# A conditioning vector loaded as eight packed columns and spread over the partitions by TensorE, with nine warming products instead of fourteen

## The chip, the cores and the metric

The kernel runs on one core of a Trainium2 chip. The metric is the device time of one execution in microseconds (us). The time before is 2213.28 us, the median of three runs that lie between 2211.96 and 2214.94 us.

## What is computed

The kernel is a trunk of two residual layers over one sequence of 1024 tokens with 1024 channels: layer 0 mixes tokens by multi-head latent attention, layer 1 by an mLSTM matrix memory, and each is followed by a gated MLP with a causal width-3 convolution. Every sub-layer normalises its input and shifts, scales and gates it by numbers that depend on a conditioning vector `c` of 1024 elements. What matters here is the head of it:

```
c_act = jax.nn.silu(c)
for i in range(DEPTH):
    mod = c_act @ mod_w[i] + mod_b[i]
    sh_a, sc_a, g_a, sh_f, sc_f, g_f = split(mod, 6)
    h = rms_norm(x) * (1 + sc_a) + sh_a
    ...  # attention or mLSTM, starting with h @ w_in
```

So no product of the first projection `h @ w_in` can be formed before the scale `sc_a` of its channels is known, and that needs `silu(c)` and the rows of `mod_w` for those channels.

## The kernel before

Activations lie with channels on the 128 partitions (P) and tokens along the free dimension, so that 1024 channels are eight tiles, counted by `k`. Products are made in three terms from a rounded high part and a rest: a helper (`mm3`, lines 171 to 182) issues high times high (L175), rest of the moving operand times high (L176) and high times rest of the weight (L177).

The first projection is made k by k, while its operands arrive. `load_k(k)` (L330 to L336) issues three DMAs on SyncE's queue: `sraw`, the 128 x 1024 block of `mod_w` that gives the scale of the channels of tile k; `wraw`, the 128 x 896 weights; and `x`, the first 512 tokens of tile k. `prepare(k)` (L338 to L345) then does, for one k:

- on VectorE (DVE) `mod_dot` (L198), which multiplies `sraw` by `crow` and sums along the row, and `mod_bias` (L203), which adds the bias column from `cols`: together they give the scale of the channels;
- on ScalarE (ACT) the rounded weights `winh` (L343), on DVE the rest `winl` (L345);
- in `scaled` on ACT the rounded scaled input (the first of the two tiles named `h`, L351), on DVE its rest (the second `h`, L352).

`in_k` (L354 to L359) issues 21 products for one k, seven output tiles `ia` times three terms. ACT also squares `x` for the normalisation (`ssq`, `sq`, L240 and L243), DVE adds the squares up (L245). The factor from the normalisation is applied only when the finished projection is read out of PSUM.

`crow` is `silu(c)` repeated on all 128 partitions, since `mod_dot` needs it along the free dimension on each. Before, a broadcast DMA (L134) writes c 128 times, 512 KB in all, as the first transfer of the program, and ACT applies the Silu in place (L135). `cols` holds small per-channel vectors (biases, gains, and so on) packed as columns; `load_cols(0, ...)` loads the first part of it (L156), from within `load_k(0)`.

Two more pieces lie in the same stretch. Fourteen products of the identity with itself (`warm`, L409) keep TensorE busy from the program's start, with no use for their result. `rope_tables` (L365 to L389) loads the positions by four small DMAs behind `load_k(1)` and works out angles with six ACT instructions (L372 to L377), DVE instructions (L378 to L382) and three sines; its result is needed only after the projection.

The order on each engine is set by a scheduler of the language's tile layer, not by hand: it may place an instruction ahead of one that is written earlier. In the trace of before each engine runs its own list from top to bottom, and an instruction that waits holds up all that stand behind it on that engine.

Of the kernel before, what the change touches and what calls it, by code (L numbers as in the profile page):

```python
# [11 lines left out]
F32 = mybir.dt.float32  # L12
F32R = mybir.dt.float32r
I32 = mybir.dt.int32
AF = mybir.ActivationFunctionType
# [3 lines left out]
P = 128  # L19
D = 1024  # L20
S = 1024
KT = D // P
HS = 512
# [16 lines left out]

STEPS = "nspppnspppoooonmooso", "nnsposppooponpmspoopo"
XW = (4, 2)
WARM = 14
W0, W0_RSTD, WF, WF_RSTD = (6, 10), (4, 3), (4, 5), (4, 4)
SHARE = 7
GATES = (2, 16, 20, 24)
# [14 lines left out]

_W = [("mb0", 48), ("mb1", 48), ("qn", 4), ("kvn", 2), ("hn", 8), ("fn", 8), ("invf", 1), ("mg", 3), ("gb", 2),
      ("cw0", 66), ("cb0", 22), ("cw1", 66), ("cb1", 22)]
COL = {}
_o = 0
# [30 lines left out]
def trunk_kernel(ctx: ExitStack, tc: tile.TileContext, xT, pos, c_d, cols_d, mod_w, win, winT, w0, w1, wf, wd, out):  # L98
    nc = tc.nc
# [3 lines left out]
    def nm(s):  # L103
        n_names[0] += 1
        return f"{s}_{n_names[0]}"

    act, dve, pool, pe = nc.scalar, nc.vector, nc.gpsimd, nc.tensor

    cst = ctx.enter_context(tc.tile_pool(name="cst", bufs=1))
# [19 lines left out]
    def block(i, shape, dt, name):  # L129
        return blk.tile(shape, dt, tag=f"b{i}", name=nm(name))  # L130


    crow = cst.tile([P, D], F32, name="crow")
    nc.sync.dma_start(crow, c_d.broadcast_to([P, D]))  # L134
    act.activation(crow, crow, AF.Silu)  # L135
    cols = [cst.tile([P, COLS[0][1]], F32, name="cols"), None, None]
    ident = cst.tile([P, P], F32, name="ident")
    make_identity(nc, ident)
# [13 lines left out]
    def load_cols(i, p):  # L152
        a, b = COLS[i]
        if i > 0:
            cols[i] = p.tile([P, b - a], F32, name=f"cols{i}")
        nc.sync.dma_start(cols[i], cols_d[:, a:b])  # L156

    def mm_tile(name):
        return psA.tile([P, HS], F32, tag="mm", name=nm(name))
# [164 lines left out]
    def load_x(hf, k):  # L324
        nc.sync.dma_start(xs[hf][:, k, :], xT[k, :, hf * HS:(hf + 1) * HS])

    def small(name):
        return psS.tile([P, HS], F32, tag="sm", bufs=1, name=nm(name))

    def load_k(k):  # L330

        nc.sync.dma_start(sraw[:, k % 4, :], mod_w[0, 8 + k])
        if k == 0:
            load_cols(0, cst)
        nc.sync.dma_start(wraw[:, k % 4, :], win[k])
        load_x(0, k)  # L336

# [27 lines left out]
    def rope_tables(scr):  # L365

        Q = S // 4
        ang, n, n1, n2, t, pi = [scr[:, i * Q:(i + 1) * Q] for i in range(6)]
        pi = pi.bitcast(I32)
        for i in range(4):  # L370
            nc.sync.dma_start(pi[32 * i:32 * i + 32, :], pos[:, i * Q:(i + 1) * Q].broadcast_to([32, Q]))
        act.activation(ang, pi, AF.Copy, scale=col("invf"))  # L372
        act.activation(n, ang, AF.Identity, scale=1.0 / TWO_PI, bias=col("mg"))
        act.activation(n, n, AF.Identity, bias=col("mg", 1))
        act.activation(n1, n, AF.Identity, scale=1.0 / 2048.0, bias=col("mg"))
        act.activation(n1, n1, AF.Identity, bias=col("mg", 1))
        act.activation(n1, n1, AF.Copy, scale=2048.0)  # L377
        dve.tensor_tensor(n2, n, n1, ALU.subtract)  # L378

        for v, part in ((n1, PI1), (n2, PI1), (n1, PI2), (n2, PI2), (n, PI3)):  # L380
            dve.scalar_tensor_tensor(ang, v, -part, ang, ALU.mult, ALU.add)
        dve.tensor_scalar(ang, ang, -PI_IN, PI_IN, ALU.max, ALU.min)  # L382
        act.activation(t, ang, AF.Abs)
        act.activation(n, t, AF.Sin, scale=-1.0, bias=col("mg", 2))
        act.activation(n1, ang, AF.Sin)
        act.activation(n2, ang, AF.Sin, scale=-1.0)
        cs_d = dram.tile([3, 4, 32, Q], F32, name="csd")
        act.dma_start(cs_d.rearrange("i q f t -> (q f) i t"), scr[:, Q:4 * Q].rearrange("p (i t) -> p i t", i=3))
        return cs_d  # L389
# [14 lines left out]
        rstd_later(ssq[hf], D, ssq[hf], keep_rb, XW[hf], small)  # L404


    ps = small("warm")
    for _ in range(WARM):
        pe.matmul(ps[:, 0:P], ident, ident, start=True, stop=True)  # L409


    load_k(0)
    load_k(1)
    cs_d = rope_tables(block(1, [P, 6 * 256], F32, "rt"))
    load_k(2)
    load_k(3)
    prepare(0)
# [405 lines left out]
    for n in range(2 * NH):  # L823
        q, kk, qr, kvu, i, hf, head = args.pop(0)
# [694 lines left out]
    for t in range(8):  # L1519
        ps = mm_tile("vp")  # L1520
# [7 lines left out]
    gi, gf, gb, gc = [g1[:, i * P:(i + 1) * P] for i in range(4)]  # L1528
# [156 lines left out]
def _units(w):  # L1685

    k, m = w.shape
    return w.reshape(k // P, P, m // P, P).transpose(2, 1, 0, 3).reshape(m // P, P, k)


def _cols(v):
    return v.reshape(-1, P).T


def arrange(inputs):
    a = {k: np.asarray(v) for k, v in inputs.items()}
    f = np.float32
    xT = np.ascontiguousarray(a["x"][0].T).reshape(KT, P, S)
    pos = np.ascontiguousarray(a["positions"][0].reshape(1, S))

    cols = np.zeros((P, NCOL), f)

    def put(name, v):
        cols[:v.shape[0], COL[name]:COL[name] + v.shape[1]] = v

    for l in range(2):
        put(f"mb{l}", _cols(a["mod_b"][l]))
        cw = a["ffn_conv_w"][l]
        put(f"cw{l}", cw.reshape(3, FT, P).transpose(2, 1, 0).reshape(P, FT * 3))
        put(f"cb{l}", _cols(a["ffn_conv_b"][l]))  # L1710
    put("qn", _cols(a["mla_q_norm"][0]))
    put("kvn", _cols(a["mla_kv_norm"][0]))
    put("hn", _cols(a["ml_head_norm"][0]))
    put("fn", _cols(a["final_norm"]))
    invf = np.array(INVF, f)
    put("invf", np.tile(invf, 4)[:, None])
    put("mg", np.tile(np.array([[MAGIC, -MAGIC, math.pi / 2]], f), (P, 1)))
    put("gb", np.repeat(a["ml_b_gates"][0].reshape(2, MH).T, NC, axis=0))

    wi = a["mla_w_in"][0]  # L1720
    win = np.concatenate([wi, wi[:, 768:]], axis=1).reshape(KT, P, 896)
    winT = np.ascontiguousarray(win.reshape(D, 896).T).reshape(7, P, D)

    mod_w = np.ascontiguousarray(a["mod_w"].transpose(0, 2, 1)).reshape(2, 48, P, D)
    wq = a["mla_w_q_up"][0].reshape(512, NH, 192)
    wkv = a["mla_w_kv_up"][0].reshape(256, NH, 256)
    w0 = np.empty((18, P, 1024), f)
    for g in range(4):
        for i in range(2):
            w0[U_QN + g, :, i * 512:(i + 1) * 512] = _units(np.ascontiguousarray(wq[:, 2 * g + i, :128]))[0]  # L1730
            w0[U_KV + g, :, i * 256:(i + 1) * 256] = _units(np.ascontiguousarray(wkv[:, 2 * g + i, :128]))[0]
        w0[U_QR + g // 2, :, (g % 2) * 512:(g % 2 + 1) * 512] = _units(
            np.concatenate([wq[:, 2 * g, 128:], wq[:, 2 * g + 1, 128:]], axis=1))[0]
        wv = np.concatenate([wkv[:, 2 * g, 128:], wkv[:, 2 * g + 1, 128:]], axis=1)
        w0[U_KV + g, :, 512:] = wv.reshape(2, P, 256).transpose(1, 0, 2).reshape(P, 512)
    w0[U_OUT0:U_OUT0 + 8] = _units(a["mla_w_out"][0])

    wm = a["ml_w_in"][0]
    w1 = np.empty((33, P, 1024), f)
    w1[U_MQ:U_MQ + 8] = _units(wm[:, 0:1024])  # L1740

    wg = np.concatenate([wm[:, 1024:1280], wm[:, 3072:]], axis=1).reshape(KT, P, 264).transpose(1, 0, 2)
    for i, u in enumerate(U_MV0):
        part = wg[:, 3 * i:3 * i + 3].reshape(P, -1)
        w1[u, :, :part.shape[1]] = part
        w1[u, :, part.shape[1]:] = 0
    for i in range(1, MH):
        wv = wm[:, 1024 + i * 256:1024 + (i + 1) * 256].reshape(2, 4, P, 256)
        w1[U_MV + 2 * i:U_MV + 2 * i + 2] = wv.transpose(0, 2, 1, 3).reshape(2, P, 1024)
    w1[U_MO:U_MO + 8] = _units(wm[:, 2048:3072])  # L1750
    w1[U_OUT1:U_OUT1 + 8] = _units(a["ml_w_out"][0])

    wf = np.empty((2, FT, 2, P, 1024), f)
    wd = np.empty((2, KT, P, FT * P), f)
    for l in range(2):
        up = _units(a["ffn_w_up"][l])
        wf[l, :, 0] = up[:FT]
        wf[l, :, 1] = up[FT:]
        wd[l] = _units(a["ffn_w_down"][l])
    return [("xT", xT), ("pos", pos), ("c", a["c"]), ("cols", cols), ("mod_w", mod_w), ("win", win),  # L1760
            ("winT", winT), ("w0", w0), ("w1", w1),
            ("wf", wf), ("wd", wd)]
# [16 lines left out]
```

## Time and profile before

| what | value |
|---|---|
| median of three runs | 2213.28 us |
| the profiled execution's own time | 2209.6 us |
| its span, first to last instruction | 2207.8 us |
| TensorE (PE) busy | 2165.6 us, 98% of the span |
| VectorE (DVE) busy | 1697.9 us, 77% |
| ScalarE (ACT) busy | 1045.3 us, 47% |
| mean granted TensorE clock | 0.996 |
| PE's share of the chain that ended last | 85% |

PE is TensorE, PEld its weight loads, SPq the queue on which SyncE issues DMAs. A line such as L198 is a line of the kernel. In a timeline the first number is the start in us from the start of the span, the second how long the row took; in brackets stands the idle time ahead of it and what ended it. The rows of a DMA issue show the issue alone; the time to landing is a view of its own. The profiled execution's time lies 1.8 us above its span and 3.7 us below the median of the three runs.

### The profile page before, as it was taken

The page shows a single profiled execution, that of the slowest core. Times are in us where ns is not written, and L with a number is a line of the kernel's source. Part 1 is how long each engine was busy: PE and PEld are TensorE (multiplying, and loading weights), DVE is VectorE, ACT ScalarE, POOL GpSimd, SP SyncE. Part 2 cuts the span into 40 slices and gives each one's busy share as a digit, 9 for nine tenths or more (in the row PEclk, how much of TensorE's full clock was granted, in tenths as well). Part 3 has the DMA queues.
Part 4 walks back from the last instruction along what each step waited for, and adds up shares of the span by engine and source line. Part 5 has one row for each costly group of instructions (what it writes and reads, how often), then busy time and mean ns, then how long its engine had stood idle before and what let it go on. Part 6 is the DMA issues. An engine that isn't in the chain of part 4 may idle for free.

```text
span 2207.8 us, 28744 instructions
## 1 busy us (share of the span) xinstructions
PE 2165.6 (98%) x10557; PEld 1817.1 (82%) x10557; DVE 1697.9 (77%) x2753; ACT 1045.3 (47%) x1812; POOL 200.5 (9%) x232
## 2 busy tenths in 40 slices
PE   9999999999999999999999999999999999999998
PEld 7878888787888888778888888988788888877887
DVE  8877788669878776999974754566887777779987
ACT  6456566456444444443353434354554444453335
POOL 0000000000000000242210111010000000022232
PEclk9999999999999999999999999999999999999999
DMA  8512334832444432543133332354233332245122
GB/s 316 156 47 67 94 102 156 278 115 74 151 143 138 134 130 80 191 150 95 51 115 105 102 124 77 114 172 158 68 134 100 110 116 95 78 155 208 45 79 77
DMA packets 105085, 270.50 MB, mean 123 GB/s; under 512 B 12336, under 2 KB 15984, under 8 KB 104944
## 3 DMA queue, kind: packets, MB, share of 16 engines
q1 hardware_dynamic: 104544, 268.28, 36.8%
q8 instruction: 83, 1.36, 0.2%
q14 instruction: 58, 0.48, 0.1%
q10 hardware_dynamic: 400, 0.39, 0.1%
HBM read 221.53 MB, written 44.47 MB: 120 GB/s over the span
## 4 chain that ended last, share of the span: by engine, by line
PE 85%; DVE 8%; DMA 2%; ACT 2%; issue 1%; POOL 0%; SPq 0%; DVEq 0%; POOLq 0%; ACTq 0%
PE pa L177 7%; PE pa L175 7%; PE pa L176 7%; PE pd L175 4%; PE pd L176 4%; PE pd L177 4%; PE sc L677 3%; PE da L175 3%; PE da L177 3%; PE da L176 3%; PE op L175 3%; PE op L177 2%; PE op L176 2%; PE inp L177 2%; PE inp L175 2%; PE db L177 2%
## 5 line engine op out<-in xcount | busy, mean ns | idle before, releaser
L992 ACT ACTIVATE whi<-raw 128x512 fp32r<-128x512 f32 (+1 forms) x252 | 147.5, 607 | 262.3 <-PE pb L176 61.0
L992 ACT ACTIVATE whi<-wsum 128x512 fp32r<-128x512 f32 (+1 forms) x224 | 133.9, 617 | 184.5 <-PE pa L176 61.5
L175 PE MATMUL pa<-T,whi 128*128 128x512 f32 x528 | 206.3, 391 | 5.0 <-DVE g L1080 5.0
L177 PE MATMUL pa<-T,wlo 128*128 128x512 f32 x528 | 206.1, 390 | 3.1 <-DVE wlo L993 3.1
L176 PE MATMUL pa<-T,whi 128*128 128x512 f32 x528 | 205.7, 390 | 0.0
L993 DVE TENSOR_TENSOR wlo<-wsum,whi 128x512 fp32r<-128x512 f32 (+1 forms) x224 | 150.6, 685 | 33.7 <-ACT whi L992 32.2
L993 POOL TENSOR_TENSOR wlo<-raw,whi 128x512 fp32r<-128x512 f32 (+1 forms) x96 | 140.8, 1480 | 382.5 <-ACT whi L992 341.8
L175 PE MATMUL da<-U,whi 128*128 128x512 f32 (+1 forms) x364 | 139.8, 384 | 2.2 <-ACT whi L992 2.2
L176 PE MATMUL da<-U,whi 128*128 128x512 f32 (+1 forms) x364 | 139.2, 382 | 0.0
L177 PE MATMUL da<-U,wlo 128*128 128x512 f32 (+1 forms) x364 | 138.5, 382 | 0.0
L167 ACT ACTIVATE whi<-wraw 128x1024 fp32r<-128x1024 f32 x67 | 70.7, 1058 | 112.7 <-PE op L176 60.2
L993 DVE TENSOR_TENSOR wlo<-raw,whi 128x512 fp32r<-128x512 f32 (+1 forms) x156 | 104.7, 678 | 24.4 <-ACT whi L992 24.4
L175 PEld LDWEIGHTS pa<-T,whi 128*128 128x128 f32 x528 | 99.3, 188 | 28.0 <-DVE g L1080 4.1
L177 PEld LDWEIGHTS pa<-T,wlo 128*128 128x128 f32 x528 | 99.3, 188 | 24.5 <-DVE wlo L993 4.0
L176 PEld LDWEIGHTS pa<-T,whi 128*128 128x128 f32 x528 | 99.3, 188 | 20.4
L1143 DVE TENSOR_TENSOR U<-q,U 128x1024 fp32r<-128x1024 f32 x84 | 108.2, 1306 | 6.0 <-ACT U L1142 5.5
L1032 ACT ACTIVATE ct<-a,cols 128x512 f32<-128x512 f32 x88 | 71.0, 808 | 87.5 <-DVE a L1054 47.8
L168 DVE TENSOR_TENSOR wlo<-wraw,whi 128x1024 fp32r<-128x1024 f32 x67 | 82.4, 1233 | 37.0 <-ACT whi L167 34.9
L177 PE MATMUL db<-U,wlo 128*128 128x512 f32 x264 | 102.7, 390 | 1.7 <-DVE wlo L993 1.7
L175 PE MATMUL db<-U,whi 128*128 128x512 f32 x264 | 103.7, 393 | 0.0
L176 PE MATMUL db<-U,whi 128*128 128x512 f32 x264 | 102.8, 390 | 0.0
L175 PE MATMUL op<-oh,whi 128*128 128x512 f32 x256 | 100.1, 391 | 1.0 <-ACT oh L731 1.0
(378 smaller groups left out, 6078.5 us busy)
## 6 DMA issues: line engine op xcount, KB each, us to landing
raw<-in_wf SPq DMA_DIRECT2D x96, 512.0 KB, 4.1
wraw<-in_w SPq DMA_DIRECT2D x67, 512.0 KB, 3.6
mraw<-in_mod_w SPq DMA_DIRECT2D x56, 512.0 KB, 3.6
ud<-ct SPq DMA_DIRECT2D x88, 256.0 KB, 2.3
q<-ud SPq DMA_DIRECT2D x88, 256.0 KB, 4.1
raw<-in_wd SPq DMA_DIRECT2D x32, 512.0 KB, 5.7
pa<-in_mod_w SPq DMA_DIRECT2D x24, 512.0 KB, 3.6
x<-xd SPq DMA_DIRECT2D x48, 256.0 KB, 4.4
```

Of the source, the lines that this page charges most:

```text
L167: act.activation(hi, raw, AF.Copy)
L168: dve.tensor_tensor(lo, raw, hi.bitcast(F32), ALU.subtract)
L175: pe.matmul(ps, lh, rh, start=first, stop=False, skip_group_check=more)
L176: pe.matmul(ps[:, 0:rl.shape[-1]], lh, rl, start=False, stop=False, skip_group_check=more)
L177: pe.matmul(ps, ll, rh, start=False, stop=last, skip_group_check=more)
L677: pe.matmul(ps[:, cs], a[:, qs if n < 3 else qrs_], b[:, cs], start=n == 0, stop=n == 4)
L992: act.activation(hi, src, AF.Copy)
L993: eng.tensor_tensor(lo, src, hi.bitcast(F32), ALU.subtract)
L1032: act.activation(t, a[:, 2:], AF.Identity, bias=col(f"cb{l}", m), scale=cw(m, 2))
L1143: dve.tensor_tensor(lo, w, hi.bitcast(F32), ALU.subtract)
```

## The change

`c` is put into the host-side array `cols` as eight columns of 128 (the table `_W` and one `put`), so that it arrives with `cols`. That load is issued first, and the broadcast of 512 KB at the program's start goes away. ACT applies the Silu to the 128 x 8 block (`ccol`). TensorE then makes `crow` in eight transposes: each takes one column, repeated along the free dimension, as a 128 x 128 operand, and writes its 128 elements as a row on all partitions of PSUM (`cr`, two tiles of four transposes). ACT copies the first half to `crow`, DVE the second. The fourteen warming products become four ahead of the transposes and five behind them, and the two `load_k` calls move ahead of them in the text. Two later broadcasts of c (L1513 and L1655) stay.

```
-WARM = 14
+WARM, WARM2 = 4, 5
...
-_W = [..., ("mg", 3), ("gb", 2),
+_W = [..., ("mg", 3), ("gb", 2), ("c", 8),
...
     crow = cst.tile([P, D], F32, name="crow")
-    nc.sync.dma_start(crow, c_d.broadcast_to([P, D]))
-    act.activation(crow, crow, AF.Silu)
...
     def load_k(k):
         nc.sync.dma_start(sraw[:, k % 4, :], mod_w[0, 8 + k])
-        if k == 0:
-            load_cols(0, cst)
         nc.sync.dma_start(wraw[:, k % 4, :], win[k])
         load_x(0, k)
...
+    load_cols(0, cst)
+    load_k(0)
+    load_k(1)
     ps = small("warm")
     for _ in range(WARM):
         pe.matmul(ps[:, 0:P], ident, ident, start=True, stop=True)
-    load_k(0)
-    load_k(1)
+    ccol = cst.tile([P, KT], F32, name="ccol")
+    act.activation(ccol, cols_at(COL["c"], KT), AF.Silu)
+    for i in range(2):
+        cr = mm_tile("cr")
+        for t in range(4):
+            pe.transpose(cr[:, t * P:(t + 1) * P], ccol[:, i * 4 + t:i * 4 + t + 1].to_broadcast([P, P]), ident)
+        if i:
+            dve.tensor_copy(crow[:, HS:], cr)
+        else:
+            act.activation(crow[:, 0:HS], cr, AF.Copy)
+    for _ in range(WARM2):
+        pe.matmul(ps[:, 0:P], ident, ident, start=True, stop=True)
     cs_d = rope_tables(block(1, [P, 6 * 256], F32, "rt"))
...
+    put("c", _cols(a["c"][0]))
```

The scheduler lays out the first stretch anew. ACT's list before, at the very start of the program (the first `winh`, `h`, `ssq` belong to tile k = 0, the second `winh` and `h` and the `sq` to k = 1, `rt` to the rope tables):

```order
L135 ACTIVATE crow<-crow 128x1024
L343 ACTIVATE winh_98<-wraw_97 128x896
L351 ACTIVATE h_94<-x_93,modc_79 128x512
L240 ACTIVATE ssq_114<-x_93 128x512
L343 ACTIVATE winh_100<-wraw_97 128x896
L351 ACTIVATE h_94<-x_93,modc_79 128x512
L243 ACTIVATE sq_195<-x_93 128x512
L372 ACTIVATE rt_138<-rt_138,cols 128x256
```

ACT's list in the changed kernel, from its first `winh`, which follows the Silu of `ccol` (line numbers stand two to four lower than before, here L339 for L343, L347 for L351, L368 to L373 for L372 to L377):

```order
L339 ACTIVATE winh_96<-wraw_95 128x896
L238 ACTIVATE ssq_112<-x_91 128x512
L339 ACTIVATE winh_98<-wraw_95 128x896
L241 ACTIVATE sq_202<-x_91 128x512
L419 ACTIVATE crow<-cr_128 128x512
L368 ACTIVATE rt_145<-rt_145,cols 128x256
L369 ACTIVATE rt_145<-rt_145,cols 128x256
L370 ACTIVATE rt_145<-rt_145,cols 128x256
L371 ACTIVATE rt_145<-rt_145,cols 128x256
L372 ACTIVATE rt_145<-rt_145,cols 128x256
L373 ACTIVATE rt_145<-rt_145 128x256
L347 ACTIVATE h_92<-x_91,modc_77 128x512
```

The copy into `crow` stands behind the weights and the squares of both k = 0 and k = 1, and the first `h` has moved from third place to behind the six rope instructions.

DVE's list before, at the same place (`modc` is the column of scales, the `h` written here is the rest of the scaled input):

```order
L198 SCALAR_TENSOR_TENSOR sraw_96,modc_79<-sraw_96,crow 128x1024
L203 SCALAR_TENSOR_TENSOR modc_79<-modc_79,cols 128x1
L345 TENSOR_TENSOR winl_99<-wraw_97,winh_98 128x896
L352 SCALAR_TENSOR_TENSOR h_95<-x_93,modc_79,h_94 128x512
L198 SCALAR_TENSOR_TENSOR sraw_96,modc_79<-sraw_96,crow 128x1024
```

DVE's list in the changed kernel, from its first instruction:

```order
L341 TENSOR_TENSOR winl_97<-wraw_95,winh_96 128x896
L341 TENSOR_TENSOR winl_99<-wraw_95,winh_98 128x896
L417 COPY crow<-cr_134 128x512
L243 TENSOR_TENSOR ssq_112<-ssq_112,sq_202 128x512
L196 SCALAR_TENSOR_TENSOR sraw_94,modc_77<-sraw_94,crow 128x1024 x2
L201 SCALAR_TENSOR_TENSOR modc_77<-modc_77,cols 128x1
L196 SCALAR_TENSOR_TENSOR sraw_94,modc_77<-sraw_94,crow 128x1024
L374 TENSOR_TENSOR rt_145<-rt_145 128x256
L377 SCALAR_TENSOR_TENSOR rt_145<-rt_145 128x256
L348 SCALAR_TENSOR_TENSOR h_93<-x_91,modc_77,h_92 128x512
```

The first scale (L201) now stands behind two weight rests, a copy, an addition of squares and two dots, where it stood behind one dot.

PE's list in the changed kernel, from its first instruction; before, fourteen `warm` were followed at once by L175, L176, L177 for each `ia` in turn:

```order
L408 MATMUL warm_121<-ident 128x128 x4
L415 MATMUL cr_128<-ident,ccol 128x128 x4
L415 MATMUL cr_134<-ident,ccol 128x128 x4
L421 MATMUL warm_121<-ident 128x128 x5
L173 MATMUL ia_181<-h_92,winh_96 128x512
L173 MATMUL ia_182<-h_92,winh_96 128x512
L173 MATMUL ia_183<-h_92,winh_96 128x512
L173 MATMUL ia_184<-h_92,winh_96 128x512
```

All seven products that need only the high part of the first `h` have moved ahead of those that need its rest. Beyond this the lists of ACT, DVE, PE and SyncE differ in some places up to the first scores of the attention, where the second half of the projection is normalised, and agree after that.

More of the change, by code (lines that the diff above doesn't have):

```diff
@@ L60 @@
 HB = ((4, 3), (1, 5))
-_W = [("mb0", 48), ("mb1", 48), ("qn", 4), ("kvn", 2), ("hn", 8), ("fn", 8), ("invf", 1), ("mg", 3), ("gb", 2),
+_W = [("mb0", 48), ("mb1", 48), ("qn", 4), ("kvn", 2), ("hn", 8), ("fn", 8), ("invf", 1), ("mg", 3), ("gb", 2), ("c", 8),
       ("cw0", 66), ("cb0", 22), ("cw1", 66), ("cb1", 22)]
```

## The prediction

> **What bounds the kernel now.** I read the page first, then the timeline of the first 20 us, then stretches of the span with their granted clock, then PE's waits. The page:
>
> ```profile
> span 2207.8 us, 28744 instructions
> PE 2165.6 (98%) x10557; PEld 1817.1 (82%) x10557; DVE 1697.9 (77%) x2753; ACT 1045.3 (47%) x1812; POOL 200.5 (9%) x232
> ```
>
> TensorE (PE) stands still for 42 us in all, so a change in the head acts only through when PE's useful work begins. The timeline shows that start (first number: start, second: length):
>
> ```profile
> 1.45 6.22 PE L409 MATMUL warm<-ident 128*128 128x128 f32 x28 [1.45 <-POOL ident masks.py:199]
> 3.91 0.44 SPq L335 DMA_DIRECT2D wraw<-in_win  x1
> 4.39 0.47 SPq L325 DMA_DIRECT2D x<-in_xT  x1
> 5.12 1.06 ACT L135 ACTIVATE crow<-crow 128x1024 f32<-128x1024 f32 x1 [3.04 <-DMA crow<-in_c]
> 6.70 1.23 DVE L198 SCALAR_TENSOR_TENSOR sraw<-sraw,crow 128x1024 f32<-128x1024 f32 x1 [6.70 <-DMA sraw<-in_mod_w]
> 7.90 0.95 ACT L343 ACTIVATE winh<-wraw 128x896 fp32r<-128x896 f32 x1 [1.73 <-DMA wraw<-in_win]
> 7.96 0.16 DVE L203 SCALAR_TENSOR_TENSOR modc<-modc,cols 128x1 f32<-128x1 f32 x1
> 8.76 0.71 ACT L351 ACTIVATE h<-x,modc 128x512 fp32r<-128x512 f32 x1
> 8.88 1.09 DVE L345 TENSOR_TENSOR winl<-wraw,winh 128x896 fp32r<-128x896 f32 x1 [0.76 <-ACT winh L343]
> 9.51 0.50 PE L175 MATMUL ia<-h,winh 128*128 128x512 f32 x1 [1.84 <-ACT h L351]
> 9.89 0.75 DVE L352 SCALAR_TENSOR_TENSOR h<-x,modc,h 128x512 fp32r<-128x512 f32 x1
> 12.46 0.63 PE L177 MATMUL ia<-h,winl 128*128 128x512 f32 x1
> 12.89 0.63 PE L175 MATMUL ia<-h,winh 128*128 128x512 f32 x1
> 16.71 0.39 PE L177 MATMUL ia<-h,winl 128*128 128x512 f32 x1
> 16.94 0.39 PE L175 MATMUL ia<-h,winh 128*128 128x512 f32 x1
> ```
>
> The Silu of c ends at 6.2 us, before the first dot starts: that dot waits for its own weights, not for c. The first product starts at 9.51, the 22nd, which opens k = 1, at 16.94. Matmul rows overlap, so their pace is the step between starts: 0.43 us at 12.5, 0.23 us at 16.8. The stretches name the reason (columns: length, PE busy and rows, granted clock, DMA share, GB/s):
>
> ```profile
> 9.51:10.80 1.29, 0.61 (x2) 1.00 1.06 401
> 10.80:14.20 3.40, 3.40 (x9) 0.50 1.03 346
> 17.00:43.00 26.00, 26.00 (x116) 1.00 0.88 321
> 43.00:100.00 57.00, 56.94 (x278) 1.00 0.59 199
> ```
>
> From 10.8 to 14.2 the clock stood at 0.50, although warming had run until 7.67: the pauses behind it cost the clock again. From 17 to 100 us PE is busy 82.94 of 83 us. So the moment at which k = 1 opens moves all that follows, one to one. About 0.2% (4.4 us) is what a measurement of this kernel can tell from no change.
>
> **The broadcast goes, and transfers land earlier.** The last loads of k = 1 are those issued at 3.91 and 4.39 (last column: us from issue to landing):
>
> ```profile
> wraw<-in_win SPq DMA_DIRECT2D x1, 448.0 KB, 7.3
> x<-in_xT SPq DMA_DIRECT2D x1, 256.0 KB, 8.0
> crow<-in_c SPq DMA_DIRECT2D x1, 512.0 KB, 4.3
> ```
>
> They land at 11.2 and 12.4. The removed 0.52 MB headed the queue in this stretch (last column again GB/s):
>
> ```profile
> 0.00:2.00 2.00, 0.55 (x2) 0.55 (x3) 0.00 (x0) 1.21 (x1) 0.77 (x8) 1.00 0.07 25
> 2.00:4.00 2.00, 2.00 (x12) 2.00 (x11) 0.00 (x0) 0.07 (x1) 0.00 (x0) 1.00 0.86 231
> ```
>
> At 231 GB/s it took 2.3 us; at the 401 GB/s of 9.51 to 10.80 it would be 1.3 us. I take 2.3, since that row is the broadcast's own: landings at 8.9 (weights) and 10.1 (x). The other end, that all 2.3 MB up to those weights flow at 401 GB/s from 2.0 us on, puts their landing at 7.7. The eight more columns in `cols` are 4 KB: nothing.
>
> **What now stands ahead of the first product.** Here the gain is lost, by the new lists. Prices not seen above:
>
> ```profile
> 13.12 0.61 ACT L243 ACTIVATE sq<-x 128x512 f32<-128x512 f32 x1
> 13.64 0.49 ACT L372 ACTIVATE rt<-rt,cols 128x256 f32<-128x256 int32 x1
> 13.93 0.69 DVE L245 TENSOR_TENSOR ssq<-ssq,sq 128x512 f32<-128x512 f32 x1
> 16.34 0.42 ACT L377 ACTIVATE rt<-rt 128x256 f32<-128x256 f32 x1
> ```
>
> ```profile
> L403 ACT ACTIVATE rbs<-rb 128x512 f32<-128x512 f32 x1 | 0.6, 599 | 0.3 <-PE rb L266 0.3
> L448 DVE TENSOR_TENSOR raw<-ia,rbs 128x512 f32<-128x512 f32 x7 | 4.7, 692 | 0.0
> ```
>
> Both halves of `crow` are read out of PSUM by engines whose lists first hold work of k = 1. On ACT the copy stands behind the second `winh` and the second square, so it can't start before the x of k = 1 has landed: 10.1 + 0.61 + 0.60 (as L403) = 11.3. On DVE it stands behind the second `winl`: 8.9 + 0.95 (`winh`) + 1.09 (`winl`) = 10.9, + 0.69 (nearest row L448, which also reads PSUM) = 11.6, + 0.69 for the addition of squares = 12.3. The first dot starts there instead of at 6.70. The scale of k = 0 follows only after two dots: 12.3 + 2 x 1.23 + 0.16 = 14.9. ACT meanwhile runs the six rope instructions from 11.3 on: 16.34 + 0.42 - 13.64 = 3.1 us, to 14.4; they hide beside the dots by 0.5 us (should the positions land over 0.5 us after the copy, the excess adds). Then `h`, 0.71: **the first product at 15.6 instead of 9.51.**
>
> Hidden: the Silu of `ccol` (nearest rows 0.16 and 0.49) and the transposes. A row of the chain has four transposes at full clock:
>
> ```profile
> 78.32 0.44 PE rb L266 x4
> ```
>
> That is 0.11 each, eight 0.9 us; the warming passes take 6.22 / 28 = 0.22 for as many columns, so at that pace 1.8 us. `cols`, now first, lands no later than the broadcast did (0.8 + 4.3 = 5.1), so `cr` is ready by 7.5 at the latest, and no copy can start before 10. The loads waited for set the time.
>
> **The clock.** Warming, transposes and the last five products end by about 7.5 us; PE then stands still for 8 us, longer than the pauses that cost it the clock before. So k = 0 starts at half pace. The half-pace stretch lasts at least the 3.4 us seen (10.8 to 14.2), and at most about 5.8, which the warming products spent at 0.22 a pass without speeding up. Half of that is lost: 1.7 to 2.9 us, I take 2.3; before, 1.7 of it is already in the 16.94. The Trainium skill ("TensorE: Matmul & The Clock Gate", Part 1) says that the gate decides in free-running windows of 3.4 us, and that one idle window throttles it again; the 3.4 us at 0.50 agrees. By it a cold start runs 3.4 to 6.8 us at half clock, which loses 2.6 us on the mean, and the sum below would be 0.3 us larger.
>
> **The sum.** k = 0 needs 21 x 0.23 = 4.8 us at full pace: k = 1 opens at 15.6 + 4.8 + 2.3 = 22.7 instead of 16.94, **5.8 us later**. PE should not starve inside k = 0: its first seven products need only the high part and last 7 x 0.43 = 3.0 us, to 18.6, while the rest of `h` follows on DVE after a dot, two rope steps (0.49 each at most, as ACT's 256-wide row) and 0.75: 14.9 + 1.23 + 0.98 + 0.75 = 17.9. At full clock this would be 0.7 us late. Each later k gives DVE 4.8 us of PE's time for 1.23 + 0.16 + 1.09 + 0.75 + 0.69 = 3.9 us of work. On the profiled execution that is 2209.6 + 5.8 = 2215.4; this execution lay 3.7 us below the median, so for the median 2213.3 + 5.8 = **2219.1 us**.
>
> Bounds: weights landing at 7.7 and 1.7 us of clock give 14.4 + 4.8 + 1.7 - 16.9 = +4.0; landing at 9.9 (only 1.3 earlier) and 2.9 give 16.6 + 4.8 + 2.9 - 16.9 = +7.4.
>
> The lists also differ where the second half is normalised, at these waits of PE:
>
> ```profile
> PE kp L175 <- ACT ckvn L499: 1.9, 1, 1.9
> PE qrp L176 <- DVE cqn L500: 0.6, 1, 0.6
> PE qrp L175 <- ACT cqn L499: 0.6, 1, 0.6
> ```
>
> In the best case these 3.1 us go; in the worst I allow as much again, in the sum nothing, for the same work stands there.
>
> **Rivals.** *The gain arrives* (faster, 0.06). If copies and dots ran as soon as their data are there, the first product would come 2.3 us earlier, at 7.2, right behind the warming work, with its clock kept: 2.3 + 1.7 = 4.0 us less, 2209.3 us. It decides at one point: whether the loads of k = 1 have landed before `cr` is ready, at 5 to 7.5 us. Up to the x of k = 1 stand 2.5 MB; between 2.0 and 7.5 that is 450 GB/s, more than the stretches above show, and otherwise the list holds the copies back. The Trainium skill (same page, Part 4) says that transposes do not count as activity for the gate; no run here shows it. By that the clock would not be kept, and this rival would win 2.3.
>
> *Absorbed* (no change, 0.24): fast loads (+4.0), or the waits of the second normalisation go (5.8 - 3.1 = +2.7): 2216.0 to 2217.3 us. For it: the DVE list wins slack against PE, as two `winl` move into its idle head. Against: PE has no waits until 100 us that slack could fill.
>
> *DVE falls behind* (slower still, 0.08): if the rest of `h` for k = 1 (behind three more rope steps, two scales and a `winl`, some 3.5 us after the first) misses the opening of k = 1, 2 to 3 us more, 2222 us.
>
> **Chances and range.** The forecast itself has 0.62; with the last rival it is slower by over 0.2%: 0.70. No change 0.24, faster 0.06. The range takes the bounds +4.0 to +7.4, the absorbed case to +2.4, the starved one to +9: 2215.7 to 2222.5.
>
> **What would show it.** Right: ACT's copy of `crow` starts behind the square of k = 1, at 10 to 12 us; the first dot near 12.3; first product near 15.6; clock 0.50 for over 3 us from there; PE without holes afterwards. Wrong: a first product before 13 us, a clock at 1.00 through k = 0, or a k = 1 that opens before 19 us; and a time under 2216 would mean that PE's later waits gave it back.

## The result, and the profile after

| | kernel before | changed kernel |
|---|---|---|
| median | 2214.11 us (2211.96 to 2215.21, 6 runs) | 2228.8 us (2223.04 to 2229.96, 6 runs) |
| ratio, with its 95% interval | | 1.0063 (1.005 to 1.0076) |
| profiled execution: time, span | 2209.6, 2207.8 us | 2229.13, 2227.4 us |
| mean granted clock in it | 0.996 | 0.990 |
| PE busy | 2165.6 us | 2179.2 us |

The change costs 14.7 us by the medians, where +5.8 was forecast. The page of the changed kernel:

```profile
span 2227.4 us, 28732 instructions
PE 2179.2 (98%) x10555; PEld 1821.4 (82%) x10555; DVE 1698.2 (76%) x2754; ACT 1046.5 (47%) x1813; POOL 201.9 (9%) x232
```

The span is 19.6 us longer, and PE is busy for 13.6 us of that, with two PE rows fewer. A later start alone would show as idle time, so PE's own work takes longer as well: by a lower clock, by slower products, or both.

First the head, in the timeline of the changed kernel (its line numbers stand two to four lower):

```profile
2.75 0.21 ACT L411 ACTIVATE ccol<-cols 128x8 f32<-128x8 f32 x1 [0.67 <-DMA cols<-in_cols]
3.33 1.91 PE L415 MATMUL cr<-ident,ccol 128*128 128x128 f32 x8
5.04 1.85 PE L421 MATMUL warm<-ident 128*128 128x128 f32 x10
10.73 0.95 ACT L339 ACTIVATE winh<-wraw 128x896 fp32r<-128x896 f32 x1 [1.99 <-DMA wraw<-in_win]
11.85 0.63 ACT L241 ACTIVATE sq<-x 128x512 f32<-128x512 f32 x1 [0.18 <-DMA x<-in_xT]
12.39 0.58 ACT L419 ACTIVATE crow<-cr 128x512 f32<-128x512 f32 x1
12.72 0.68 DVE L417 COPY crow<-cr 128x512 f32<-128x512 f32 x1
13.92 1.22 DVE L196 SCALAR_TENSOR_TENSOR sraw<-sraw,crow 128x1024 f32<-128x1024 f32 x1
16.21 0.16 DVE L201 SCALAR_TENSOR_TENSOR modc<-modc,cols 128x1 f32<-128x1 f32 x1
16.40 0.72 ACT L347 ACTIVATE h<-x,modc 128x512 fp32r<-128x512 f32 x1 [0.41 <-DVE modc L201]
17.17 3.36 PE L173 MATMUL ia<-h,winh 128*128 128x512 f32 x7 [10.29 <-ACT h L347]
24.92 0.39 PE L173 MATMUL ia<-h,winh 128*128 128x512 f32 x1
```

The transposes are done at 5.24, but both copies wait behind work of k = 1: ACT stands 1.99 us for that k's weights, until 10.73, and then takes `crow` behind the square, and DVE takes its half behind `winl`. So `cr` lies ready for 7 us. The first product starts at 17.17 (9.51 before) and k = 1 opens at 24.92 (16.94 before): **8.0 us later**. The stretches from there (length, PE, PEld, DVE, ACT, POOL, granted clock, DMA share, GB/s):

```profile
17.17:23.30 6.13, 6.13 (x14) 4.84 (x15) 6.13 (x16) 4.43 (x8) 0.00 (x0) 0.50 1.00 379
25.00:43.00 18.00, 18.00 (x80) 14.77 (x79) 18.00 (x32) 13.17 (x22) 0.00 (x0) 1.00 0.97 360
43.00:104.00 61.00, 60.85 (x295) 50.04 (x294) 49.91 (x89) 21.00 (x31) 4.95 (x4) 1.00 0.52 161
1146.30:1149.70 3.40, 3.40 (x10) 2.68 (x9) 3.40 (x6) 1.45 (x2) 0.00 (x0) 0.50 0.00 0
```

The clock stands at 0.50 for 6.13 us from the first product on, then PE runs almost without holes to 104 us. The last row is one of four single stretches of 3.4 us at half clock that this execution has between 500 us and its last 10 us; the profiled execution of before had one there. The Trainium skill ("TensorE: Matmul & The Clock Gate", Part 1) tells of free-running windows of 3.4 us; the length agrees. Three stretches more lose about 5 us by estimate, and the mean clock differs between runs of one kernel (0.990 to 0.994 in those of the changed kernel), so the two medians are a better account than the two profiles.

Now PE's own work. In the MLP 24 products read one tile `T` (T1 in the code), the next 24 a tile `B` (B22), the next 24 a `T` again (T2). The first product of each in the timeline of the kernel before:

```profile
508.60 0.39 PE L175 MATMUL pd<-T,whi 128*128 128x512 f32 x1
514.04 0.39 PE L175 MATMUL pd<-B,whi 128*128 128x512 f32 x1
519.48 0.39 PE L175 MATMUL pa<-T,whi 128*128 128x512 f32 x1
```

The same three in the changed kernel:

```profile
516.60 0.39 PE L173 MATMUL pd<-T,whi 128*128 128x512 f32 x1
522.04 0.39 PE L173 MATMUL pd<-B,whi 128*128 128x512 f32 x1
527.64 0.39 PE L173 MATMUL pa<-T,whi 128*128 128x512 f32 x1
```

Matmul rows overlap, so the step between starts is the pace. Before, both blocks of 24 take 5.44 us, 226.7 ns a product. After, the block on `T` still takes 5.44, but that on `B` takes 5.60: 233.3 ns. The same holds for all products on B22 and T3, 1052 of them: 6.6 ns each is 6.9 us. Over all 512-wide products at full clock (steps with a pause in them left out), what lies above 226.7 ns sums to 3.9 us before and 12.7 us after. Both instruction streams are the same in this stretch. What differs is where the tiles lie (byte addresses within a partition, from the two built programs):

| tile | before | after |
|---|---|---|
| `whi`, first buffer (weights) | 113376 | 113440 |
| T1 | 88800 | 88864 |
| B22 | 176096 | 176096 |
| T3 | 192480 | 192480 |

`cols` grew by eight columns, 32 bytes a partition, and `ccol` adds another 32. All that is laid out behind them from the left moves by 64 bytes, the weights among it; B22 and T3 lie in a pool that is laid out from the right and stay. The distance from weights to B22 was 62720, 245 times 256; now it is 62656, 192 over a multiple of 256.

### The profile page after: what moved, and what is told of

It reads as the page before. It is cut to its first block, busy times and chain, and to the rows that moved or that the text cites. A ratio compares the mean times of both kernels' runs of the same rounds, so it can differ in the third digit from the quotient of the medians.

```text
span 2227.4 us, 28732 instructions
## 1 busy us (share of the span) xinstructions
PE 2179.2 (98%) x10555; PEld 1821.4 (82%) x10555; DVE 1698.2 (76%) x2754; ACT 1046.5 (47%) x1813; POOL 201.9 (9%) x232
## 4 chain that ended last, share of the span: by engine, by line
PE 86%; DVE 7%; DMA 3%; ACT 2%; issue 2%; POOL 1%; SPq 0%; DVEq 0%; POOLq 0%; ACTq 0%
PE pa L175 7%; PE pa L173 7%; PE pa L174 7%; PE pd L173 4%; PE pd L174 4%; PE pd L175 4%; PE da L173 3%; PE da L175 3%; PE da L174 3%; PE sc L687 3%; PE op L173 2%; PE op L175 2%; PE op L174 2%; PE db L175 2%; PE db L173 2%; PE db L174 2%
## 5 line engine op out<-in xcount | busy, mean ns | idle before, releaser
L175 PE MATMUL pa<-T,wlo 128*128 128x512 f32 x528 | 207.1, 392 | 3.1 <-DVE wlo L1003 3.1
L175 PE MATMUL da<-U,wlo 128*128 128x512 f32 (+1 forms) x364 | 138.5, 382 | 0.0
L175 PEld LDWEIGHTS pa<-T,wlo 128*128 128x128 f32 x528 | 99.3, 188 | 26.1 <-DVE wlo L1003 4.0
L175 PE MATMUL db<-U,wlo 128*128 128x512 f32 x264 | 102.7, 390 | 1.7 <-DVE wlo L1003 1.7
L173 PE MATMUL inp<-h,whi 128*128 128x512 f32 x256 | 102.1, 399 | 0.0
```

The lines of the kernel that those rows point to most:

```text
L173: pe.matmul(ps, lh, rh, start=first, stop=False, skip_group_check=more)
L175: pe.matmul(ps, ll, rh, start=False, stop=last, skip_group_check=more)
```

## The experiments

**The theory:** two causes that add up, the late head and the 64 bytes. **The rivals:** the longer products come of the new order or of the clock; or any shift costs, whatever its size.

**One: the kernel before, shifted by 64 bytes.** An unused tile behind the two `modc` tiles; the same instructions in the same order.

```
     modc = [cst.tile([P, 48], F32, name=f"modc{i}") for i in range(2)]
+    pad = cst.tile([P, 16], F32, name="pad")
```

> The kernel before with an unused tile of 64 bytes per partition among the constants; every instruction as before. Theory A (the 64 bytes by which the new column tile and the wider cols push all tiles behind them set weights and moving operand of the MLP's B22 and T3 products apart by 64 bytes modulo 128, which costs such a product 6.5 ns): 1052 products x 6.5 ns and some of T2, so 7 to 8 us slower, near 2222 us, and products on B22 and T3 at 233 ns a step. Theory B (the slower products come from the new order of instructions, or from the clock): the same time as before, 2214 us, with steps of 227 ns.

Measured: 2220.06 us against 2210.17 of the kernel before beside it, ratio 1.0043 (1.0029 to 1.0057). Its three blocks:

```profile
509.35 0.39 PE L176 MATMUL pd<-T,whi 128*128 128x512 f32 x1
514.79 0.39 PE L176 MATMUL pd<-B,whi 128*128 128x512 f32 x1
520.39 0.39 PE L176 MATMUL pa<-T,whi 128*128 128x512 f32 x1
```

5.44 us on `T`, 5.60 on `B`, as in the changed kernel, without any of its instructions. So neither the new order nor c's new way lengthens the products; an unused tile of 64 bytes does, and costs 9.9 us (6.4 to 12.6 by the interval). The steps account for it: what lies above 226.7 ns sums to about 9.5 us more than in the kernel before.

**Two to four: other shifts.** The kernel before with a pad of 128 bytes and of 32 bytes, and the changed kernel with a pad of 64, so that it is shifted by 128 in all.

> The kernel before with an unused tile of 128 bytes per partition. Theory A with a period of 128 bytes: as before, 2214 us, steps of 227 ns on B22 and T3. If the period is 256 bytes or more: 7 to 8 us slower. Theory B: 2214 us.

> The kernel before with an unused tile of 32 bytes per partition. Theory A: between 2214 and 2222 us; it tells whether only a distance of 64 bytes costs (then 2214) or any distance that is no multiple of 128 (then 2222). Theory B: 2214 us.

> The changed kernel with an unused tile of 64 bytes per partition, which makes the whole shift 128 bytes. Theory A: 7 to 8 us faster than the changed kernel, near 2221 us, which leaves the late first product (about 8 us at the opening of k = 1) as the whole rest; steps on B22 and T3 back at 227 ns. Theory B: as the changed kernel, near 2229 us.

Measured, against the same 2210.17: 2221.8 us, ratio 1.0047 (1.0034 to 1.0059); 2224.17 us, 1.0058 (1.0046 to 1.0071); 2224.43 us, 1.0061 (1.0049 to 1.0074). Mean steps on B22 and T3: 232.7, 233.5 and 232.7 ns. A shift of 128 bytes doesn't bring the pace back, so the theory's first form, a period of 128 bytes, is wrong: if there is a period, it is longer. The fourth run shows neither the 227 ns nor the time near 2221 us that this form gave; it is not told apart from the changed kernel by its time.

**Five and six: a shift of 256 bytes.** The changed kernel with a pad of 192 bytes, so that it is shifted by 256 in all, and the kernel before with a pad of 256.

```
+    pad = cst.tile([P, 48], F32, name="pad")     # the changed kernel
+    pad = cst.tile([P, 64], F32, name="pad")     # the kernel before
```

> The changed kernel with an unused tile of 192 bytes per partition behind the two small modc tiles, so that the tiles on the left side stand 256 bytes further on than in the kernel before, instead of 64; the same instructions in the same order. Theory A (the pace of a 128x512 product depends on how far the moving operand's address lies from the weights' address, and a distance that is no multiple of 256 bytes costs some 6 ns): the mean step of the products on the two tiles of the right-hand pool goes from 233.3 ns back to 227, the excess of all steps over 226.7 ns from 12.7 us to about 4, and the time to about 8 to 9 us under the changed kernel's, some 8 us over the kernel before (the late head alone), a ratio near 1.004. Rival B (the longer products come of the other order of the head, or of the clock): steps stay at 233 ns, the time stays 14 us or more over the kernel before. Rival C (any shift from the layout before costs, whatever its size): also 233 ns. The first product stays at about 17.2 us and the products of k=1 open at about 25 us by all three.

> The kernel before with an unused tile of 256 bytes per partition, so that the left side's tiles shift by 256 bytes; the same instructions. Theory A: distances are again multiples of 256, steps 227 ns, time the same as before within 0.15%. Rival C (any shift costs): as with shifts of 32, 64 and 128 bytes, 10 to 14 us slower, steps 233 ns.

Measured: the changed kernel 2217.51 us against 2212.19, ratio 1.0024 (1.0015 to 1.0034); the kernel before 2213.17, ratio 1.0002 (0.9994 to 1.0011). The three blocks of the changed kernel with 192 bytes:

```profile
515.36 0.39 PE L174 MATMUL pd<-T,whi 128*128 128x512 f32 x1
520.80 0.39 PE L174 MATMUL pd<-B,whi 128*128 128x512 f32 x1
526.24 0.39 PE L174 MATMUL pa<-T,whi 128*128 128x512 f32 x1
```

5.44 and 5.44 us: the pace is back, the sum above 226.7 ns is 3.6 us, and the shift of the kernel before costs nothing that can be measured. Both rivals fall. Over the eight kernels so far:

| kernel | distance B22 to weights, modulo 256 | step on B22 and T3, ns |
|---|---|---|
| before; before + 256; changed + 192 | 0 | 226.7 to 226.8 |
| before + 128; changed + 64 | 128 | 232.7 |
| changed; before + 64 | 192 | 233.3 |
| before + 32 | 224 | 233.5 |

The two causes add up within the noise: 9.9 us for the 64 bytes (run one) and 5.3 us for the change without them (run five) make 15.2, each known to 2 or 3 us; the change cost 14.7. In run five the first product came at 17.35 and k = 1 opened at 24.82, 7.9 us later than before, yet the end is only 5.3 later (3.3 to 7.5 by the interval): in its profile, PE's waits of over 0.25 us at `rb`, `qrp`, `kp`, `qp` and `op` between 104 and 402 us, 4.9 us in the kernel before, shrink to 2.9, and the rest is within the interval. Why these waits shrink is not shown.

**Seven: the head in the order of the text.** The changed kernel with 192 bytes, and all of the head pinned: copies of `crow`, then for each k the dot, the bias, `winh`, `h`, its rest, `winl`, the squares; the row dots too. The rope table comes behind `h` of k = 1.

```
-            act.activation(crow[:, 0:HS], cr, AF.Copy)
+            tc.keep_in_program_order(act.activation(crow[:, 0:HS], cr, AF.Copy))
...
-        mod_dot(0, 8 + k, sraw[:, k % 4, :])
-        mod_bias(0, 8 + k)
-        act.activation(hi, raw, AF.Copy)
+        pin = tc.keep_in_program_order
+        pin(mod_dot(0, 8 + k, sraw[:, k % 4, :]))
+        pin(mod_bias(0, 8 + k))
+        pin(act.activation(hi, raw, AF.Copy))
...
-    cs_d = rope_tables(block(1, [P, 6 * 256], F32, "rt"))
```

> The changed kernel with the same 192 bytes of padding, and with its head held in the order of the program on ACT and DVE: the two copies of c's row, then for each k the dot, the bias, the weights' rounding, h and its rest, the squares; the rope table's steps come behind the scaled rows of k=1 and k=2 instead of ahead of those of k=0. If the late head came from the order in which ACT and DVE take the copies, the rope steps and the second load (the theory): copies at about 5 us, first dot at about 5.7, first product at 7.5 to 9 (17.2 in the changed kernel, 9.5 before), products of k=1 open at 13 to 17, and the time 0 to 6 us under the kernel before, ratio 0.997 to 1.000. If instead the broadcast by TensorE itself is late (transposes or the copies out of PSUM take longer than shown): first product after 11 us and a time over the kernel before by 2 us or more. If loads are the bound at k=1 whatever the order: first product early, k=1 still at 17 or later, time within 0.1% of before.

Measured: first product 8.45, k = 1 at 13.40, both better than the kernel before, and yet 2223.32 us, ratio 1.0053 (1.0039 to 1.0066), where up to 6 us less had been expected. Some of PE's waits in it (in brackets, idle time and what ended it):

```profile
26.05 1.51 PE L175 MATMUL ia<-h,winh 128*128 128x512 f32 x4 [2.24 <-ACT h L350]
59.47 0.50 PE L176 MATMUL ia<-h,winh 128*128 128x512 f32 x1 [1.27 <-DVE h L351]
104.67 0.50 PE L175 MATMUL qrp<-cqn,whi 128*128 128x512 f32 x1 [2.23 <-DVE raw L467]
127.39 0.80 PE L175 MATMUL kp<-ckvn,whi 128*128 128x512 f32 x1 [1.93 <-ACT ckvn L521]
```

This `kp` starts at 127.39, 12 us later than in the kernel before:

```profile
115.40 0.50 PE L175 MATMUL kp<-ckvn,whi 128*128 128x512 f32 x1 [1.93 <-ACT ckvn L499]
```

So the 1.93 us at `kp` are not of the pinning. The wait that ends at 26.05 is: a dot of k = 3 stood behind the whole rope table on DVE. At 59.47 the rest of `h` stood behind a row dot and the seven reads out of PSUM on DVE, and at 104.67 `raw` came late while DVE was busy all of 98 to 104 us; how much of these is due to the pinned row dots and squares is not separated. The head was mended, and the fixed order cost more behind it; in runs eight and nine, with less of it, the time is back near that of the kernel before.

**Eight and nine: only the first k's held.** Pinned are k = 0 and 1 (eight), or 0 to 2 (nine); what is written behind may only be issued behind them, and is otherwise left to the scheduler.

```
+            if k == PIN - 2:
+                for i in last:
+                    behind.enter_context(tc.issue_after(i.ins))
+                cs_d = next(rope)
```

> The changed kernel with 192 bytes of padding, in which only k=0 and k=1 of the head are held in the program's order on ACT and DVE (copies of c's row, dot, bias, the weights' rounding, h and its rest); all that is written behind them, the rope table too, may be issued only after them and is otherwise ordered by the scheduler, as in the changed kernel. In the run that held all eight k's and the row dots in order, the first product came at 8.45 us and k=1 opened at 13.2, but PE stood 2.24 us at 23.8 for a dot of k=3 queued behind the rope table on DVE, and later at 51 to 59 and 101 to 105 us. Theory (the fixed order behind the head gave the gain back): with k=2 on free again, first product 8.5 us, k=1 at 13 to 13.5, less than 1 us of holes from 25 to 104 us, and the first of the kp products by 112 to 114 us (115.4 before, 122.5 in the changed kernel with 192 bytes); time 1 to 5 us under the kernel before. Here h of k=2 stands behind the weights of k=3 on ACT, which may cost a hole of some 2 us at 18 us. Rival (DVE, busy 10.0 of 10 us from 18 to 68 us in the kernel before, is the bound there, and an earlier start of PE only waits for it later): holes of 3 us or more come back between 18 and 70 us, time within 0.15% of the kernel before.

> As the run that holds k=0 and k=1, but with k=2 held in order too, and the rope table's steps behind it. Theory: first product 8.5 us, k=1 at 13 to 13.5, no hole at 18 us (h of k=2 no longer stands behind the weights of k=3), kp by 111 to 113 us, time 2 to 6 us under the kernel before and at or under the run with two. Rival (DVE is the bound from 18 to 68 us): as there, holes of 3 us or more and a time within 0.15% of before.

Measured: 2213.16 us against 2213.25, ratio 1.0006 (0.9997 to 1.0015), and 2215.85, ratio 1.0013 (1.0004 to 1.0022). The head of run eight:

```profile
4.42 0.60 ACT L424 ACTIVATE crow<-cr 128x512 f32<-128x512 f32 x1 [1.40 <-PE cr L420]
5.28 0.69 DVE L422 COPY crow<-cr 128x512 f32<-128x512 f32 x1 [5.28 <-PE cr L420]
8.61 1.20 PE L175 MATMUL ia<-h,winh 128*128 128x512 f32 x4 [1.71 <-ACT h L350]
13.52 0.39 PE L175 MATMUL ia<-h,winh 128*128 128x512 f32 x1
19.30 1.89 PE L175 MATMUL ia<-h,winh 128*128 128x512 f32 x7 [0.84 <-ACT h L350]
30.47 0.97 PE L175 MATMUL ia<-h,winh 128*128 128x512 f32 x3 [1.18 <-ACT h L350]
46.65 0.65 PE L266 MATMUL rb<-ident,rstd 128*128 128x128 f32 x4 [0.55 <-POOL rstd L259]
```

Its stretches from there, with the same columns as above:

```profile
8.00:13.50 5.50, 4.89 (x21) 4.03 (x22) 4.08 (x7) 3.82 (x7) 0.00 (x0) 1.00 1.04 369
13.50:28.00 14.50, 13.66 (x59) 10.69 (x58) 13.71 (x27) 9.47 (x16) 0.00 (x0) 1.00 1.03 402
28.00:48.00 20.00, 18.28 (x85) 14.54 (x84) 16.57 (x32) 13.66 (x24) 1.02 (x1) 1.00 0.84 312
48.00:68.00 20.00, 19.99 (x92) 16.04 (x92) 20.00 (x40) 4.41 (x7) 0.00 (x0) 1.00 0.64 232
```

And the kernel before there:

```profile
18.00:28.00 10.00, 10.00 (x46) 8.29 (x45) 10.00 (x20) 6.83 (x13) 0.00 (x0) 1.00 1.04 402
28.00:48.00 20.00, 19.94 (x94) 16.37 (x94) 19.70 (x35) 15.32 (x25) 1.85 (x1) 1.00 0.84 301
```

Copies at 4.42 and 5.28, first product at 8.61, clock at 1.00 up to 68 us, k = 1 at 13.52: c by TensorE puts the head 3.4 us ahead of the kernel before. Of that, PE loses 0.84 us of the 14.5 up to 28 us and 1.72 of the 20 up to 48. ACT's rows show why:

```profile
17.29 0.96 ACT L342 ACTIVATE winh<-wraw 128x896 fp32r<-128x896 f32 x1 [0.82 <-DMA wraw<-in_win]
18.54 0.70 ACT L350 ACTIVATE h<-x,modc 128x512 fp32r<-128x512 f32 x1
27.54 0.96 ACT L342 ACTIVATE winh<-wraw 128x896 fp32r<-128x896 f32 x1 [2.47 <-DMA wraw<-in_win]
29.71 0.70 ACT L350 ACTIVATE h<-x,modc 128x512 fp32r<-128x512 f32 x1
```

Both times the `h` that PE waits for stands behind the rounding of weights that hadn't landed, and the second time behind four rope instructions too. The last 0.9 us of the lead are gone by the first `kp` product of all (98.10 us against 97.98); where they go is not traced. The `kp` product that waits 1.93 us then starts at 117.44, behind another stretch at half clock around 105 us, which costs up to 1.7 us, against 115.40 before. None of the 1 to 6 us that the theory gave came, nor its `kp` by 114 us, and run nine is even a little slower than before. The rival named DVE as the bound. Its time came (within 0.15%), its holes of 3 us or more between 18 and 70 us did not (2.6 us in run eight, 1.7 in run nine); DVE is in fact less busy from 28 to 48 us than before (16.57 of 20 against 19.70), and the larger holes shown are ended by ACT's `h`. So the place of most of the loss is shown, and the rival's reason for it isn't. No version beat the kernel before; run eight equals it.

## Why the prediction was wrong

The sign and the mechanism in the head were right, the size was not, and some two thirds of the loss (9.9 of 15.2 us) came from a cause that the prediction had dismissed.

- *"`cols` are 4 KB: nothing."* **This is the step that failed.** As a transfer it is nothing: `cols` landed by 2.75. As a tile it moves every address behind it by 32 bytes, `ccol` by another 32, and the 1052 products on two tiles that don't move take 233.3 instead of 226.7 ns. Alone that costs 9.9 us (run one), and the pace comes back with 192 more unused bytes (run five).
- *Weights of k = 1 at 8.9, x at 10.1.* Mis-sized. The two loads of the changed kernel that were issued at 3.13 and 3.68 took (last column)

```profile
wraw<-in_win SPq DMA_DIRECT2D x1, 448.0 KB, 7.6
x<-in_xT SPq DMA_DIRECT2D x1, 256.0 KB, 8.2
```

  to land: 10.7 and 11.9, only 0.5 us earlier than before, not 2.3. I credited the removed broadcast at the slow 231 GB/s of its own stretch. The bound of 1.3 that I kept was still too much. From 5 to 8 us the transfers of the changed kernel ran at 266 to 290 GB/s, those of the kernel before at 354 to 386; why stays open.
- *Copy on ACT done at 11.3, first dot at 12.3, first product at 15.6.* The order was right, and each is late by about what the landing is late: 12.97 (started at 12.39, where 10 to 12 had been named), 13.92 and 17.17, so +1.6 at the product. The timeline shows the copies behind k = 1's loads, and `h` waiting last for its scale behind two dots (0.41 us, `modc`), with the rope steps hidden beside them as forecast. Runs seven and eight show that this order alone makes the head late: with the copies ahead the first product comes at 8.45 and 8.61.
- *Clock loss 2.3 us.* The stretch at 0.50 lasted 6.13 us from the first product on, longer than the 5.8 that were taken as the most: 3.1 us lost, so +0.8. With +1.6, and k = 0 in itself 0.1 shorter, this makes the head about 8.0 instead of 5.8 us late, past the upper bound of 7.4. That the time without the 64 bytes came out at +5.3 us (run five), near the forecast, is partly luck: a head that was later than worked out, and waits behind it that shrank.
- *PE without holes afterwards.* Right: 60.85 of 61 us from 43 to 104. "In the sum nothing" for the second normalisation was nearly right: of its three waits, 3.1 us, one at `qrp` went, 0.6 us; those at `kp` and at the other `qrp` stayed (run five).
- *The rival that the gain arrives* needed copies that run as soon as `cr` is ready. Where that was arranged, the head gained 3.4 us (4.0 had been worked out), the clock held at 1.00 through transposes and warming, and the gain was gone by the `kp` products. So a gain in the head didn't move all that follows "one to one": 2.5 us of it went in holes by 48 us, most of them behind ACT's `h`. That sentence of the prediction holds up to 104 us for the delay of the changed kernel, and only in part beyond (7.9 us at k = 1, 5.3 in the time of run five).

In the profile 13.6 of the 19.6 us are PE busy time. The prediction had looked at when PE starts and at its clock in the first k, and had taken the pace of all later products for given.

## What to carry to other kernels

An edit that adds a few bytes to an early tile moves every tile behind it: print the addresses of what TensorE reads before and after, and keep the distance of moving operand and weights as it was, with an unused tile if need be. Where a broadcast or a load is made cheaper, look at what stands ahead of its consumers in each engine's list, since data that are ready 7 us early are worth nothing there. When a kernel gets slower, first split the difference into PE idle and PE busy. If busy time grows with the same products, look at the granted clock, and then compare the steps of the same products at full clock: what is left there is no matter of waits.

## What the runs showed of the hardware

- The pace of 128x512 products depends on where the moving operand lies relative to tiles laid out with the weights: 226.7 ns where the distance to the weights is a multiple of 256 bytes, 232.7 to 233.5 ns where it is 128, 192 or 224 over one. Products on T1 and T4, which move along with the weights, stay at 226.7 to 227.0 ns in all eight kernels, and the products on B22 change with B22 where it was; so it is the distance and not either address. Those on T2, which moves along too, have 226.7 ns on the mean where the distance of B22 is a multiple of 256 and 227.8 to 228.5 in the other five kernels. In the block of the changed kernel that opens at 527.64 only the second to fifth step, right behind the products on B22, are longer (236, 229, 232 and 231 ns), and from the sixth on they take 226 to 227; why the first ones are long is not shown. Other distances were not tried on B22 and T3, and nothing here tells which access meets which (the weights are the tile that TensorE reads beside the operand, but all left-side tiles moved together).
- At half clock the products start 0.43 us apart, and the clock came back only after 6.13 us of them; single stretches of 3.4 us at 0.50 also fall in the middle of the program, some with PE busy for all of it (1146.30 to 1149.70). Behind 500 us the eleven profiled executions have one to five of them each, leaving out the last 10 us, mostly at the same few places of the program (538.7 us in the changed kernel and 538.3 in run five, 1598.0 in the kernel before and 1598.2 in run six), but not all places each time. They can explain much of why runs of one kernel spread by 2 to 8 us: the fastest run of the changed kernel, 2223.04 us, had a mean clock of 0.994, the slowest, 2229.96, one of 0.990; over 2225 us that difference is worth up to 9 us by estimate.
